# A triangular inverse by sixteen-row blocks in a hybrid decoder layer

## Chip, cores and metric

The kernel runs on one core of a Trainium2 chip. The metric is device time in microseconds of one execution; lower is better. TensorE is called PE, VectorE DVE, ScalarE ACT, GpSimd POOL, and SyncE, which issues most DMAs, SP.

## What is computed

One layer of a decoder with three parallel mixers (A: gated DeltaNet, B: RG-LRU, C: gated linear attention) between a common input projection and a common output projection, then a gated feed-forward block; 2048 prompt tokens and 64 sample tokens, float32. The change lies in mixer A, which treats chunks of 64 tokens for each of six heads:

```python
kk = jnp.einsum('bhid,bhjd->bhij', ki, ki)
lhs = eye + bi[..., :, None] * kk * dec_strict            # 64 x 64, unit lower triangular
rhs = jnp.concatenate([bi[..., None] * vi, (bi * jnp.exp(gcum))[..., None] * ki], axis=-1)
sol = lax.linalg.triangular_solve(lhs, rhs, left_side=True, lower=True, unit_diagonal=True)
u, wk = sol[..., :dv], sol[..., dv:]
w = u - jnp.einsum('bhik,bhkv->bhiv', wk, S)
qk = jnp.einsum('bhid,bhjd->bhij', qi, ki) * dec_incl
o = jnp.exp(gcum)[..., None] * jnp.einsum('bhik,bhkv->bhiv', qi, S) + jnp.einsum('bhij,bhjv->bhiv', qk, w)
S_new = jnp.exp(g_last)[..., None] * S + jnp.einsum('bhjk,bhjv->bhkv', k_dec, w)   # to the next chunk
```

## The kernel before

The program runs in stretches: the input projection (matmuls into `pm`, to about 530 us), mixer A, mixer C beside the output projection, and the feed-forward block.

Mixer A (`deltanet`) takes its 33 chunks (32 of the prompt, one that holds the 64 sample tokens) in nine batches: eight of four chunks and the sample batch. Batches go in pairs; the last pair has the sample batch as a third member. For each pair the program is written as: `prep` of its batches, `inverse` of the pair, `ahead` (some steps of the gates' projection), `blocks` of its batches, then for each batch `tokens`, `weights` and `chain`.

- `prep`: chunk decays (PE `pcl`, line 792 and 797), exponents (PE `pa`, DVE `ex`, ACT `ex` and `eb`), and for each pair of heads the scores (PE `pk`, line 837), which DVE multiplies into `LT` (the strictly triangular matrix L, line 839) and `R` (line 842). Loads of keys and queries (`kq`, `kbd`) are issued on SP one batch ahead.
- `inverse`: ACT copies the 32 x 32 diagonal blocks of L to `X0` (named `Xd`, line 888), DVE transposes them so that each partition (a lane) holds one 32 x 32 block (`Y`, line 891). Then forward substitution: in step j a column of L times row j of the result (`tmp`, line 895) is subtracted from the rows below (`Tm`, line 897). It takes 31 steps of two DVE instructions; a pair has 96 blocks of 32 rows, 24 on each group of 32 partitions (27 in the last pair), which are called quadrants here. Two transposes give the inverse back with rows on partitions in both orientations: `Tt`, which is the tile `Y` again (line 898), and `Ut` (line 899). Then PE multiplies the off-diagonal block with it (`pp`, line 906) and ACT copies the product to `Ps`.

```python
for j in range(31):
    k = 31 - j
    t = tmp[:, :k * (j + 1)].rearrange("p (a b) -> p a b", a=k)
    nc.vector.tensor_tensor(t, Y[:, j + 1:, j:j + 1].to_broadcast([128, k, j + 1]),
                            Tm[:, j:j + 1, :j + 1].to_broadcast([128, k, j + 1]), op=OP.mult)
    nc.vector.tensor_tensor(Tm[:, j + 1:, :j + 1], Tm[:, j + 1:, :j + 1], t, op=OP.subtract)
nc.vector.transpose(Tt, Tm.rearrange("p i j -> p j i"))
nc.vector.transpose(Ut.rearrange("p a b -> p (a b)"), Tm.rearrange("p a b -> p (a b)"))
```

- `blocks`: ACT copies `Ut` into `WU` (line 920), PE makes the block off the diagonal (`pu`, line 930), ACT copies it (line 934).
- `tokens`: PE transposes keys and values (`pt`, `pv`), DVE scales them to `KB`, `KD` and `X`. `weights`: PE `pw` (line 944), ACT to `WU`.
- `chain`: the recurrence. For each chunk PE `cw` (line 962), an ACT copy to `X` (line 963), PE `cw` (line 965), an ACT copy to the next chunk's `X` (line 972); then the output `po`. For every two chunks a head norm follows, an alternation of DVE (`ob`, `z`, `e`), ACT (`z`) and PE (`po` with `ones`).

Beside all this `gates` projects the gates of mixers A and C: 1152 matmuls into `zp` (lines 1121 to 1123), whose operands are loaded by SP, split by ACT (`xh`) and POOL (`xl`, line 1089). They have no tie to the inverse and fill PE.

The order of the work on each engine in mixer A is not written out by hand. A scheduler lays the program's instructions out before the launch, by their place in the program and its own costs, and each engine then runs its list in order. PSUM has eight banks; tiles with the tag "t" (`pp`, `pu`, `pt`, `pv`, `pw`) share two of them, `zp` has one.

Of the kernel before, what the change touches and what calls it, by code (L numbers as in the profile page):

```python
# [16 lines left out]
T = 2048  # L17
# [82 lines left out]
def _build_consts():  # L100
    """Selectors and masks that follow from the shapes."""
# [21 lines left out]
    add("lns", lns)  # L123
    add("lnb", lns * EPS)
# [10 lines left out]
    # sixteen of each 32 rows are kept; selA and selB take both parts of split rows  # L135
# [4 lines left out]
    # token-major columns: 0-2 -C of head 2p | 3-5 -C of head 2p+1 | 6-11 ln beta  # L140
    # | 12-17 A | 18-23 gl-g+lrk
# [39 lines left out]
def pack(inp):  # L181
    """Lay the inputs out for the chip: permutations, transposes and zero padding only."""
# [84 lines left out]
# ---------------------------------------------------------------- the chip  # L267
# [45 lines left out]
def mm3(nc, ps, wh, wl, xh, xl, first=True, last=True, by_k=False):  # L313
    """float32 product from three single passes over exactly split operands (lists over K)."""
    n = len(wh)
    seq = [(wh, xh), (wl, xh), (wh, xl)]
    order = [(a, k) for k in range(n) for a in range(3)] if by_k else [(a, k) for a in range(3) for k in range(n)]
    for i, (a, k) in enumerate(order):
        w, x = seq[a]
        nc.tensor.matmul(ps, w[k], x[k], start=first and i == 0, stop=last and i == 3 * n - 1)  # L320


def phase1(E):
    nc, tc, s, col = E.nc, E.tc, E.s, E.col
    with ExitStack() as ctx:
# [24 lines left out]
        def first_w():  # L350
            """the first tile in two parts, the second beside the first of the tokens"""
# [32 lines left out]
        def log1p(u, e, t, w):  # L384
            """u = ln(1 + e) for 0 <= e <= 1 with the rounding of 1 + e made good; t, w scratch"""
# [78 lines left out]
        def post_packed():  # L464
            """rates and decays of mixer A, a row for each head and block of tokens"""
# [56 lines left out]
        def conv(ps, nb, key, sst, ocol, taps, bias):  # L522
            """causal width-4 convolution of a block; returns a [128, n] tile"""
# [184 lines left out]
def deltanet(E, ctx, pools, need, ahead):  # L708
    """Gated DeltaNet: chunks of 64 tokens, all six heads. Operands are made for batches of four chunks,
    the triangular systems are solved for two batches at once."""  # L710
# [15 lines left out]
    LTs = [pool.tile([128, 3, 2 * CH + 1, 64], F32, name=f"LT{i}") for i in range(2)]  # L726
    X0 = inv.tile([128, 32, 32], F32, name="Xd")
    Y = inv.tile([128, 32, 32], F32, name="Y")
    Tm = inv.tile([128, 32, 32], F32, name="Tm")
    tmp = inv.tile([128, 16 * 17], F32, name="tmp")  # L730
    Ut, Tt = inv.tile([128, 32, 32], F32, name="Ut"), Y
# [50 lines left out]
    def shared(g):  # L782
        """per-token columns and chunk decays"""
# [30 lines left out]
    def decay(g, p):  # L814
        """exponents of the decay between tokens of a chunk, masked"""
# [28 lines left out]
    def prep(g):  # L844
        """decays and scores of a batch"""
# [6 lines left out]
    def tokens(g):  # L852
        """keys and values with tokens on the partitions"""
# [25 lines left out]
    def inverse(gs):  # L879
        """U = ((I + L)^-1)^T per chunk and head; 32 x 32 diagonal blocks by substitution, a lane each,  # L880
        and the first product for the block off the diagonal"""
# [3 lines left out]
        for q in range(4):  # L885
            r = slice(q * 32, (q + 1) * 32)
# [3 lines left out]
        nc.gpsimd.memset(Tm.rearrange("p a b -> p (a b)")[:, ::33], 1.0)  # L890
        nc.vector.transpose(Y.rearrange("p a b -> p (a b)"), X0.rearrange("p a b -> p (a b)"))
        for j in range(31):
            k = 31 - j
            t = tmp[:, :k * (j + 1)].rearrange("p (a b) -> p a b", a=k)
            nc.vector.tensor_tensor(t, Y[:, j + 1:, j:j + 1].to_broadcast([128, k, j + 1]),  # L895
                                    Tm[:, j:j + 1, :j + 1].to_broadcast([128, k, j + 1]), op=OP.mult)
            nc.vector.tensor_tensor(Tm[:, j + 1:, :j + 1], Tm[:, j + 1:, :j + 1], t, op=OP.subtract)  # L897
        nc.vector.transpose(Tt, Tm.rearrange("p i j -> p j i"))
        nc.vector.transpose(Ut.rearrange("p a b -> p (a b)"), Tm.rearrange("p a b -> p (a b)"))
# [12 lines left out]
    def blocks(g):  # L912
        """U of a batch, with its block off the diagonal"""
# [23 lines left out]
    def weights(g):  # L937
        """products of U with the keys"""
# [8 lines left out]
    def outputs(t0):  # L947
        """where the outputs of 128 tokens gather, and their gates"""
# [83 lines left out]
    C = load_consts(E, early, ["selC", "selG", "mneg", "mnegs"])  # L1032
# [38 lines left out]
def gates(E, ctx):  # L1071
    """The gates of mixers A and C before their activation; a generator of steps."""
# [10 lines left out]
    def split(h, lo, src, name):  # L1083
        """src from memory into rounded parts"""
# [82 lines left out]
def ln_stats(E, r, m, mv, st):  # L1167
    """mean and variance of the rows of r[:m] to mv[:m]"""
# [6 lines left out]
def ln_scale(E, mv, m):  # L1175
    """variances in mv[:m, ..., 1] to the factors of the layer norm"""
# [18 lines left out]
def head_norm(E, tr, po, z, gain, ones, out):  # L1195
    """out = RMS norm over each head of the rows of po, times silu(z); po and z are overwritten. The gate's
    sigmoid is exp(-ln(1 + exp(-z))), and the two logarithms share one exponential."""
# [15 lines left out]
class Gla:  # L1213
    """Gated linear attention: chunks of 64 tokens, six heads, operands made for four chunks at a time.
# [757 lines left out]
```

## Time and profile before

| | |
|---|---|
| runs, us | 3038.8, 3035.73, 3043.57; median 3038.8 |
| span of the profiled execution, us | 3039.2 |
| profiled execution's own time, us | 3039.2 (the profile gives its span alone) |
| mixer A in the trace, us | about 535 to 1012 |
| substitution (lines 895, 897) in the trace, us | first step 577.0, last 877.2 |

The profile is one execution of the program on the chip. Its lines name engine, line of the program, operation and tiles (out<-in). A wait is put down to what ended last before it. Every float32 matmul appears as two records, with a weight load each; a `zp` product is one.

### The profile page before, as it was taken

To read this page: it belongs to the slowest core of one execution; us is meant where nothing else is said; L and a number is where in the kernel's file an instruction comes from. 1 tells how busy PE (TensorE), PEld (TensorE's weight loads), DVE (VectorE), ACT (ScalarE), POOL (GpSimd) and SP (SyncE) were. 2 spreads that over 40 slices of the span, in tenths; PEclk is the share of its full clock that TensorE was granted. 3 is DMA by queue.
4 is the path that set the end of the run, shared out by engine and by line. 5 is a ranking of instruction groups with operands and counts; after the bars stand their busy time and mean duration, and the time that the engine had idled before them with its cause. 6 is when DMAs were issued, how large, how long until landed. Compare 5 with 4: busy or idle time off the path is not lost.

```text
span 3039.2 us, 44833 instructions
## 1 busy us (share of the span) xinstructions
PE 2895.7 (95%) x17755; PEld 2496.9 (82%) x17755; DVE 1597.9 (53%) x2654; ACT 1231.6 (41%) x2591; POOL 843.4 (28%) x892
## 2 busy tenths in 40 slices
PE   8999999789889899998899999999999999999998
PEld 7888789678778677776678888888889999999997
DVE  4564442587665688978533333333366444334446
ACT  4474443446665567756332222222232222222223
POOL 0000001734523545434322222222232222222224
PEclk9999999689898679999999999999999999999999
DMA  6221112433433333322431111111124111111111
GB/s 197 83 74 70 56 61 100 137 106 107 123 99 91 81 120 109 111 82 87 160 123 50 49 42 63 42 56 42 49 104 152 42 47 51 49 42 42 48 43 62
DMA packets 182106, 247.20 MB, mean 81 GB/s; under 512 B 37986, under 2 KB 147640, under 8 KB 181832
## 3 DMA queue, kind: packets, MB, share of 16 engines
q1 hardware_dynamic: 179768, 237.02, 24.2%
q0 software_dynamic: 1984, 7.12, 0.6%
q8 instruction: 140, 2.29, 0.3%
q14 instruction: 70, 0.57, 0.1%
q10 hardware_dynamic: 144, 0.20, 0.0%
HBM read 183.94 MB, written 60.08 MB: 80 GB/s over the span
## 4 chain that ended last, share of the span: by engine, by line
PE 79%; DVE 10%; ACT 4%; issue 3%; DMA 2%; POOL 2%; SPq 0%; POOLq 0%; ACTq 0%; DVEq 0%
PE pm L320 20%; PE pd L320 15%; PE pug L320 15%; PE puv L320 15%; PE s L1364 2%; PE zp L1121 1%; DVE Tm L897 1%; DVE y L1779 1%; DVE tmp L895 1%; DVE K L1337 1%; PE zp L1122 1%; ACT WU L920 1%; PE zp L1123 1%; PE pd L1861 1%; DMA fxl<-s_x1T 1%
## 5 line engine op out<-in xcount | busy, mean ns | idle before, releaser
L1715 DVE SCALAR_TENSOR_TENSOR act<-G,cols,act 128x1024 f32<-128x1024 f32 (+1 forms) x132 | 123.6, 950 | 493.5 <-ACT act L1713 491.1
L1868 DVE TENSOR_TENSOR y<-y,pd 128x512 f32<-128x512 f32 x322 | 220.9, 687 | 203.3 <-PE pd L320 196.8
L1606 POOL TENSOR_TENSOR wl_d<-ws_d,wh_d 128x1024 fp32r<-128x1024 f32 x44 | 106.2, 2415 | 571.3 <-ACT wh_d L1605 547.3
L320 PE MATMUL pd<-wh_d,hh 128*128 128x512 f32 x704 | 215.8, 391 | 4.4 <-DVE y L1868 2.6
L320 PE MATMUL pd<-wh_d,hl 128*128 128x512 f32 x704 | 215.4, 391 | 0.0
L320 PE MATMUL pd<-wl_d,hh 128*128 128x512 f32 x704 | 214.9, 390 | 0.0
L1695 ACT COPY G<-pug 128x512 f32<-128x512 f32 (+2 forms) x110 | 55.2, 503 | 386.3 <-PE pug L320 386.3
L320 PE MATMUL pug<-fxh,wh_g 128*128 128x512 f32 (+2 forms) x880 | 197.0, 352 | 5.3 <-ACT fxh L1658 2.7
L320 PE MATMUL pug<-fxl,wh_g 128*128 128x512 f32 (+2 forms) x880 | 196.6, 352 | 2.5 <-POOL fxl L1659 1.5
L320 PE MATMUL puv<-fxh,wl_v 128*128 128x512 f32 (+2 forms) x880 | 197.1, 353 | 1.1 <-POOL wl_v L1606 1.1
L320 PE MATMUL puv<-fxh,wh_v 128*128 128x512 f32 (+2 forms) x880 | 197.1, 353 | 0.0
L320 PE MATMUL puv<-fxl,wh_v 128*128 128x512 f32 (+2 forms) x880 | 196.9, 352 | 0.0
L320 PE MATMUL pug<-fxh,wl_g 128*128 128x512 f32 (+2 forms) x880 | 196.2, 352 | 0.3 <-POOL wl_g L1606 0.3
L320 PE MATMUL pm<-xh,wh 128*128 128x448 f32 (+1 forms) x800 | 181.9, 360 | 8.3 <-ACT xh L370 6.7
L1605 ACT CAST wh_d<-ws_d 128x1024 fp32r<-128x1024 f32 x44 | 45.7, 1039 | 339.1 <-PE pd L1861 174.9
L320 PE MATMUL pm<-xh,wl 128*128 128x448 f32 (+1 forms) x800 | 181.7, 359 | 0.0
L320 PE MATMUL pm<-xl,wh 128*128 128x448 f32 (+1 forms) x800 | 180.0, 358 | 0.1
L1757 DVE TENSOR_TENSOR hl<-act,hh 128x512 fp32r<-128x512 f32 (+2 forms) x110 | 124.1, 1128 | 99.5 <-ACT hh L1749 99.5
L320 PEld LDWEIGHTS pug<-fxh,wh_g 128*128 128x128 f32 x880 | 156.2, 188 | 21.7 <-ACT fxh L1658 4.3
L320 PEld LDWEIGHTS pug<-fxl,wh_g 128*128 128x128 f32 x880 | 155.7, 188 | 16.9 <-POOL fxl L1659 2.0
L320 PEld LDWEIGHTS puv<-fxh,wl_v 128*128 128x128 f32 x880 | 156.1, 189 | 15.3 <-POOL wl_v L1606 1.3
L320 PEld LDWEIGHTS pm<-xh,wh 128*128 128x128 f32 x800 | 144.6, 188 | 28.9 <-issue 10.1
(731 smaller groups left out, 6371.0 us busy)
## 6 DMA issues: line engine op xcount, KB each, us to landing
ws_d<-in_w_dn SPq DMA_DIRECT2D x44, 512.0 KB
ws_g<-in_w_up SPq DMA_DIRECT2D x43, 512.0 KB
ws_v<-in_w_up SPq DMA_DIRECT2D x43, 512.0 KB
zx<-in_xT SPq DMA_DIRECT2D x56, 256.0 KB
ws<-in_w_in SPq DMA_DIRECT2D x19, 512.0 KB
x<-in_x SPq DMA_DIRECT2D x16, 512.0 KB
s_x<-x SPq DMA_DIRECT2D x16, 512.0 KB
s_x1T<-xt SPq DMA_DIRECT2D x16, 512.0 KB
```

Of the source, the lines that this page charges most:

```text
L320: nc.tensor.matmul(ps, w[k], x[k], start=first and i == 0, stop=last and i == 3 * n - 1)
L895: nc.vector.tensor_tensor(t, Y[:, j + 1:, j:j + 1].to_broadcast([128, k, j + 1]), Tm[:, j:j + 1, :j + 1].to_broadcast([128, k, j + 1]), op ...
L897: nc.vector.tensor_tensor(Tm[:, j + 1:, :j + 1], Tm[:, j + 1:, :j + 1], t, op=OP.subtract)
L920: nc.scalar.copy(o[:, h, :, :, jh * 32:(jh + 1) * 32], Ut[r, :, :3 * mt].rearrange("p i (a c) -> p a c i", a=3)[:, :, g.c0:g.c0 + m])
L1121: nc.tensor.matmul(ps, wh[:, k], xl, start=k == 0, stop=False)
L1364: nc.tensor.matmul(ps[64:, c], K[:, i], Q[:, i], start=True, stop=True)
L1605: nc.scalar.copy(h, t)
L1606: nc.gpsimd.tensor_tensor(lo, t, h.bitcast(F32), op=OP.subtract)
L1695: nc.scalar.copy(G[:, 2 + o:2 + o + m], p[:, :m])
L1715: nc.vector.scalar_tensor_tensor(dst(act), src(i), taps[i], dst(act), op0=OP.mult, op1=OP.add)
L1757: nc.vector.tensor_tensor(dst, act[:, c], hh[:, c].bitcast(F32), op=OP.subtract)
L1868: nc.vector.tensor_tensor(y, y, ps, op=OP.add)
```

## The change

Each block of 32 rows is taken as two blocks of sixteen on its diagonal and one block of sixteen by sixteen below them. With D for the inverse of the two diagonal blocks (zero elsewhere) and N for the lower block, the inverse of the 32 rows is D - D N D. The substitution runs on both blocks of sixteen at once in the same lane, in 15 steps of two DVE instructions. D N is a round of small matmuls into `pn`, copied by ACT to `Wd` (the tile `Tm`), and its product with D is made in both orientations (`pb` for `Ut`, `pc` for `Tt`), to be subtracted by three DVE instructions. `X0` is kept for N: ACT scales its upper half of columns by a mask (`half`, one more constant to load), POOL clears the other half.

The tiles `Y` and `Tm` get 32 more elements for each lane, so that the view `diagonal` can step from one block to the other. Comments and docstrings are gone from the whole program, which moves line numbers.

```diff
+    def square(t):
+        return t[:, :1024].rearrange("p (a b) -> p a b", b=32)
+    def diagonal(t):
+        return t.rearrange("p (b x) -> p b x", b=2)[:, :, :512].rearrange("p b (i j) -> p b i j", j=32)[:, :, :, :16]
-    Y = inv.tile([128, 32, 32], F32, name="Y")
-    Tm = inv.tile([128, 32, 32], F32, name="Tm")
-    tmp = inv.tile([128, 16 * 17], F32, name="tmp")
-    Ut, Tt = inv.tile([128, 32, 32], F32, name="Ut"), Y
+    Yf = inv.tile([128, 2 * 528], F32, name="Y")
+    Tf = inv.tile([128, 2 * 528], F32, name="Tm")
+    Y, Tm, Yb, Tb = square(Yf), square(Tf), diagonal(Yf), diagonal(Tf)
+    tmp = inv.tile([128, 2 * 64], F32, name="tmp")
+    Ut, Tt, Wd = inv.tile([128, 32, 32], F32, name="Ut"), Y, Tm
...
+        quads = [slice(q * 32, (q + 1) * 32) for q in range(4)]
...
-        for j in range(31):
-            k = 31 - j
-            t = tmp[:, :k * (j + 1)].rearrange("p (a b) -> p a b", a=k)
-            nc.vector.tensor_tensor(t, Y[:, j + 1:, j:j + 1].to_broadcast([128, k, j + 1]),
-                                    Tm[:, j:j + 1, :j + 1].to_broadcast([128, k, j + 1]), op=OP.mult)
-            nc.vector.tensor_tensor(Tm[:, j + 1:, :j + 1], Tm[:, j + 1:, :j + 1], t, op=OP.subtract)
+        nc.scalar.activation(X0[:, 16:], X0[:, 16:], AF.Copy, scale=C["half"])
+        nc.gpsimd.memset(X0[:, :16], 0.0)
+        for j in range(15):
+            k = 15 - j
+            t = tmp[:, :2 * k * (j + 1)].rearrange("p (b i j) -> p b i j", b=2, i=k)
+            sh = [128, 2, k, j + 1]
+            nc.vector.tensor_tensor(t, Yb[:, :, j + 1:, j:j + 1].to_broadcast(sh),
+                                    Tb[:, :, j:j + 1, :j + 1].to_broadcast(sh), op=OP.mult)
+            nc.vector.tensor_tensor(Tb[:, :, j + 1:, :j + 1], Tb[:, :, j + 1:, :j + 1], t, op=OP.subtract)
         nc.vector.transpose(Tt, Tm.rearrange("p i j -> p j i"))
-        nc.vector.transpose(Ut.rearrange("p a b -> p (a b)"), Tm.rearrange("p a b -> p (a b)"))
+        nc.vector.transpose(Ut.rearrange("p a b -> p (a b)"), Tf[:, :1024])
+        for u0 in range(0, ns, 16):
+            w = min(16, ns - u0)
+            pn = psum(f"pn{gs[0].b}{u0}", (128, 16, 32), "t")
+            for u in range(w):
+                for r in quads:
+                    nc.tensor.matmul(pn[r, u], X0[r, :, u0 + u], Tt[r, :, u0 + u], start=True, stop=True)
+            nc.scalar.copy(Wd[:, u0:u0 + w], pn[:, :w])
+        pb = psum(f"pb{gs[0].b}", (128, 32, 16), "t")
+        for u in range(ns):
+            for r in quads:
+                nc.tensor.matmul(pb[r, u], Wd[r, u], Ut[r, 16:, u], start=True, stop=True)
+        pc = psum(f"pc{gs[0].b}", (128, 32, 16), "t")
+        for u in range(ns):
+            for r in quads[::2]:
+                nc.tensor.matmul(pc[r, u], Ut[r, :, u], Wd[r, u, :16], start=True, stop=True)
+        for r in quads[::2]:
+            nc.vector.tensor_tensor(Tt[r, :16, :ns], Tt[r, :16, :ns], pc[r, :ns].rearrange("p u j -> p j u"),
+                                    op=OP.subtract)
+        nc.vector.tensor_tensor(Ut[:, 16:, :ns], Ut[:, 16:, :ns], pb[:, :ns].rearrange("p u i -> p i u"),
+                                op=OP.subtract)
...
-    C = load_consts(E, early, ["selC", "selG", "mneg", "mnegs"])
+    C = load_consts(E, early, ["selC", "selG", "mneg", "mnegs", "half"])
```

The scheduler then lays the whole of mixer A out anew. In the rows that follow, each is line, operation, tiles and shape of what is written, with `x16` for sixteen equal ones in a row; numbers behind a name tell buffers apart. In the changed kernel lines are 9 to 33 higher than before (`ex` is line 831, `pk` 846, `pp` 939, `cw` 995 and 998).

PE at the first inverse. Before, `pp` follows a run of `zp`, of which 234 stand ahead of it:

```order
L1123 MATMUL zp_0_5912<-xh_2_5891,zh_4334 128x256
L906 MATMUL pp_4773<-Y,LT_4435 32x32 x16
L906 MATMUL pp_4792<-Y,LT_4435 32x32 x16
L1121 MATMUL zp_0_5912<-xl_3_5904,zh_4334 128x256
L1122 MATMUL zp_0_5912<-xh_3_5903,zl_4335 128x256
```

Now 150 `zp` stand ahead of `pn` (and 168 ahead of `pp`):

```order
L846 MATMUL pk_5866<-kq_5771,kbd_4432 128x128 x4
L918 MATMUL pn_4745<-Y,Xd 32x32 x64
L918 MATMUL pn_4811<-Y,Xd 32x32 x32
L1154 MATMUL zp_0_5582<-xl_1_5550,zh_4334 128x256
...
L1154 MATMUL zp_0_5582<-xl_2_5562,zh_4334 128x256
L923 MATMUL pb_4845<-Ut,Tm 32x16 x96
L927 MATMUL pc_4942<-Tm,Ut 32x16 x48
```

So 84 `zp` and 16 of the 56 `pk` that stood ahead of the end of the first substitution have moved behind it.

PE at the end of the first pair's chain, beside which the second inverse runs. Before, the second inverse's `pp` and `pu` stand within the chain (`cw`):

```order
L965 MATMUL cw_5167<-X_4421,KD_4423 64x64 x6
L977 MATMUL po_5143<-R_4416,X_4421 64x64 x6
L906 MATMUL pp_5775<-Y,LT_4436 32x32 x16
L906 MATMUL pp_5794<-Y,LT_4436 32x32 x16
...
L819 MATMUL pa_6927<-rs_6850,sel 128x256 x2
L962 MATMUL cw_5391<-X_4422,WU_4426 64x64 x6
L906 MATMUL pp_5813<-Y,LT_4436 32x32 x16
L930 MATMUL pu_6296<-Ut,Ps 32x32 x16
```

Now `pn`, `pb` and `pc` stand there, and `pp` behind the chain's last `cw`:

```order
L923 MATMUL pb_6066<-Ut,Tm 32x16 x13
L927 MATMUL pc_6163<-Tm,Ut 32x16 x10
L998 MATMUL cw_5691<-X_4422,KD_4424 64x64 x6
L1010 MATMUL po_5667<-R_4417,X_4422 64x64 x6
L927 MATMUL pc_6163<-Tm,Ut 32x16 x29
L1239 MATMUL po_5667<-z_5668,c_ones 128x384
L927 MATMUL pc_6163<-Tm,Ut 32x16 x9
...
L846 MATMUL pk_7354<-kq_7259,kbd_4433 128x128 x4
L828 MATMUL pa_7367<-rs_7290,sel 128x256 x2
L939 MATMUL pp_6215<-Y,LT_4436 32x32 x16
```

The second half of the chain has no `zp` beside it any more; `pp`, `pu`, the next pair's `prep` and the tokens of the pair itself come after it.

DVE at the same place. Before, the transposes that end the second inverse stand ahead of the chain's second norm (`ob`, `z`, `e`):

```order
L897 TENSOR_TENSOR Tm<-Tm,tmp 128x31
L898 STREAM_TRANSPOSE Y<-Tm 128x1024
L899 STREAM_TRANSPOSE Ut<-Tm 128x1024
L842 TENSOR_TENSOR R_4416<-pk_6891,ex_6884 64x256 x2
L842 TENSOR_TENSOR R_4416<-pk_6914,ex_6907 64x256 x2
L1204 TENSOR_TENSOR ob_5188<-po_5143,z_5144 128x384
```

Now the subtractions that end it stand within the chain's fourth and last norm:

```order
L1237 TENSOR_TENSOR ob_5712<-po_5667,z_5668 128x384
L1241 SCALAR_TENSOR_TENSOR z_5668<-e,z_5668 128x384
L929 TENSOR_TENSOR Y<-Y,pc_6163 32x16x24 x2
L931 TENSOR_TENSOR Ut<-Ut,pb_6066 128x16x24
L1234 TENSOR_SCALAR e<-z_6880 128x384
```

Its transposes come 25 rows earlier, ahead of the first norm; the subtractions have moved behind the last one's `z`, which waits for ACT.

More of the change, by code (lines that the diff above doesn't have):

```diff
@@ L123, in _build_consts @@
     add("lns", lns)
+    add("half", p % 32 < 16)
     add("lnb", lns * EPS)
@@ L884, in inverse @@
         LT = gs[0].LT
-        for q in range(4):
-            r = slice(q * 32, (q + 1) * 32)
+        quads = [slice(q * 32, (q + 1) * 32) for q in range(4)]
+        for q, r in enumerate(quads):
             o = (q % 2) * 32
@@ L889, in inverse @@
         nc.gpsimd.memset(Tm, 0.0)
-        nc.gpsimd.memset(Tm.rearrange("p a b -> p (a b)")[:, ::33], 1.0)
-        nc.vector.transpose(Y.rearrange("p a b -> p (a b)"), X0.rearrange("p a b -> p (a b)"))
-        for j in range(31):
-            k = 31 - j
-            t = tmp[:, :k * (j + 1)].rearrange("p (a b) -> p a b", a=k)
-            nc.vector.tensor_tensor(t, Y[:, j + 1:, j:j + 1].to_broadcast([128, k, j + 1]),
-                                    Tm[:, j:j + 1, :j + 1].to_broadcast([128, k, j + 1]), op=OP.mult)
-            nc.vector.tensor_tensor(Tm[:, j + 1:, :j + 1], Tm[:, j + 1:, :j + 1], t, op=OP.subtract)
@@ L898, in inverse @@
-        nc.vector.transpose(Tt, Tm.rearrange("p i j -> p j i"))
-        nc.vector.transpose(Ut.rearrange("p a b -> p (a b)"), Tm.rearrange("p a b -> p (a b)"))
+        nc.gpsimd.memset(Tf[:, :1024:33], 1.0)
+        nc.vector.transpose(Yf[:, :1024], X0.rearrange("p a b -> p (a b)"))
+        nc.scalar.activation(X0[:, 16:], X0[:, 16:], AF.Copy, scale=C["half"])
[7 more added lines that the diff above has]
+            nc.vector.tensor_tensor(Tb[:, :, j + 1:, :j + 1], Tb[:, :, j + 1:, :j + 1], t, op=OP.subtract)
```

## The prediction

> **What bounds the kernel now.** I read the page first, then the busy time by stage, then the chain of waits in three stages, then single rows.
>
> ```profile
> span 3039.2 us, 44833 instructions
> PE 2895.7 (95%) x17755; PEld 2496.9 (82%) x17755; DVE 1597.9 (53%) x2654; ACT 1231.6 (41%) x2591; POOL 843.4 (28%) x892
> ```
>
> Over the whole span PE is the bound. The change lies in mixer A, about 535 to 1012 us, so that stretch decides. I cut it where the state chain of each pair of batches issues its first cw matmul: 667.0, 742.6, 833.3 and 928.0 us. This view gives busy time by stage; the seven stages are called P, I, B and 0 to 3 here.
>
> ```profile
> core 0: us, PE busy (x) PEld busy (x) DVE busy (x) ACT busy (x) POOL busy (x), PEclk, DMA share, GB/s
> 535.00:575.00 40.00, 30.54 (x192) 28.56 (x192) 11.73 (x25) 18.73 (x36) 31.15 (x33) 0.63 0.54 154
> 575.00:632.00 57.00, 40.97 (x284) 38.17 (x284) 51.30 (x92) 23.95 (x50) 32.79 (x37) 0.79 0.40 115
> 632.00:667.00 35.00, 31.45 (x392) 28.65 (x392) 26.58 (x57) 19.42 (x42) 10.53 (x12) 0.80 0.32 93
> 667.00:742.60 75.60, 70.94 (x883) 63.43 (x881) 51.40 (x96) 48.91 (x95) 27.25 (x27) 0.95 0.35 99
> 742.60:833.30 90.70, 78.17 (x902) 70.13 (x901) 68.87 (x124) 58.11 (x118) 47.56 (x66) 0.89 0.43 123
> 833.30:928.00 94.70, 84.61 (x952) 74.73 (x951) 63.45 (x138) 59.59 (x160) 31.13 (x40) 0.92 0.37 105
> 928.00:1012.00 84.00, 79.91 (x785) 69.93 (x784) 33.83 (x70) 41.29 (x119) 31.08 (x33) 0.88 0.27 77
> ```
>
> Two things are to be seen. In stage I (the first inverse) DVE is busy 51.3 of 57 us and PE stands for 16 us: DVE is the bound. In stages 0 to 2 PE is busy 70.9 of 75.6, 78.2 of 90.7 and 84.6 of 94.7 us, so it stands for 4.7 + 12.5 + 10.1 = 27.3 us only, although DVE is loaded too. The chain of waits says how much of those stages the substitution (lines 895 and 897) holds:
>
> ```profile
> by line: ACT WU L920 9.1%; DVE Tm L897 8.3%; ACT Xd L888 8.1%; PE zp L1121 7.2%; PE cw L962 6.9%; PE zp L1122 6.3%; DVE tmp L895 6.1%; PE zp L1123 6.0%; PE pw L944 4.6%; PE pk L837 4.1%; PE cw L965 3.1%; PE po L1206 3.1%; PE pu L930 3.0%; P
> by line: ACT WU L920 7.6%; ACT Xd L888 7.4%; DVE Tm L897 6.7%; issue 6.1%; PE pw L944 5.8%; PE zp L1121 5.2%; PE cw L965 5.0%; PE zp L1122 5.0%; PE cw L962 4.8%; PE zp L1123 4.6%; DVE tmp L895 4.0%; PE pu L930 3.4%; PE pt L870 3.0%; DMA zx<
> by line: DVE tmp L895 12.0%; DVE Tm L897 11.4%; issue 7.5%; PE zp L1121 6.7%; ACT WU L920 6.4%; PE zp L1122 5.4%; PE zp L1123 5.3%; PE cw L962 3.5%; DMA q<-s_cq 3.5%; PE cw L965 2.6%; DVE KB L871 2.2%; DVE X L877 2.1%; DVE KD L872 1.9%; DVE
> ```
>
> These are stages 0, 1 and 2: 14.4% of 75.6, 10.7% of 90.7 and 23.4% of 94.7 us, which is 10.9 + 9.7 + 22.2 = 42.8 us.
>
> **The change part by part.** *Substitution.* By line, and four rows of the view that keeps shapes apart:
>
> ```profile
> L895 DVE TENSOR_TENSOR tmp<-Y,Tm 128x31 f32<-128x31 f32 (+15 forms) x124 | 67.1, 541 | 3.6
> L897 DVE TENSOR_TENSOR Tm<-Tm,tmp 128x31 f32<-128x31 f32 (+15 forms) x124 | 64.3, 519 | 3.6
> L895 DVE TENSOR_TENSOR tmp<-Y,Tm 128x112 f32<-128x112 f32 x8 | 5.2, 644 | 0.2
> L897 DVE TENSOR_TENSOR Tm<-Tm,tmp 128x112 f32<-128x112 f32 x8 | 3.1, 392 | 0.2
> L895 DVE TENSOR_TENSOR tmp<-Y,Tm 128x87 f32<-128x87 f32 x8 | 2.1, 257 | 0.2
> L897 DVE TENSOR_TENSOR Tm<-Tm,tmp 128x87 f32<-128x87 f32 x8 | 2.0, 249 | 0.2
> ```
>
> Now: (67.1 + 64.3) / 4 = 32.9 us for each of four inverses, in 62 instructions. After: 30 instructions of 30 to 128 elements, 91 in the mean, which lies between the last four rows; their mean is 386 ns, so 30 x 0.386 = 11.6 us.
>
> *First inverse, on the path.* The time at which it ends now, and the first cw:
>
> ```profile
> 630.14 1.92 DVE L898 STREAM_TRANSPOSE Y<-Tm 128x1024 f32<-128x1024 f32 x1
> 631.98 1.20 DVE L899 STREAM_TRANSPOSE Ut<-Tm 128x1024 f32<-128x1024 f32 x1
> 632.11 1.98 PE L906 MATMUL pp<-Y,LT 32*32 32x32 f32 x64 [2.94 <-DVE Y L898]
> 667.04 0.45 PE L962 MATMUL cw<-X,WU 128*64 128x64 f32 x4
> 592.83 0.41 DVE L839 TENSOR_TENSOR LT<-pk,ex 128x256 f32<-128x256 f32 x1
> ```
>
> In the new DVE order an LT product of the next pair, the one that ran at 592.8, stands ahead of the last seven steps. It waits for a pk that the change does not hasten, so I leave it there: 592.8 + 1.3 (LT and R) + 7 x 0.39 + 3.1 (transposes) = 600. Then come pn, its copy, pb and pc, priced below at 3.8 + 0.7 + 3.8 + 3.0, and three subtractions. Their nearest row is a DVE product from PSUM with as many columns:
>
> ```profile
> L1204 DVE TENSOR_TENSOR ob<-po,z 128x384 f32<-128x384 f32 x14 | 7.7, 550 | 12.9 <-PE po L977 10.3 <-DMA s_mix<-ob 2.5
> ```
>
> 3 x 0.55 = 1.7, and with a microsecond and a half of hand-overs the first pp comes at 614.5 instead of 632.1: a gain of 17.6 us. Bounds: 9, with small matmuls at the higher price below (4.4 more) and hand-overs of 2 us; 21, with the lower price and steps of 0.25 us.
>
> *The new small matmuls.* Nearest row: pp above, whose loop alternates two heads on two 32x32 tiles: 1.98 us for 64 records, 31 ns each (a program's matmul is two records). pn and pb alternate four quadrants. Bounds: 31 ns, if four go no faster than two, and 15, if they go twice as fast. I take 20, nearer to the second, because the loop is of the same kind, only wider. An inverse has 2 x 192 records of pn and pb and 96 of pc on two quadrants: 384 x 0.020 + 96 x 0.031 = 10.7 us, between 8.8 and 14.9; the last one, with 27 systems, 12.0. [...] No row here shows four side by side.
>
> *Moved zp products* (the gates' projection, filler on PE). How many ran in each stage from I on:
>
> ```profile
> 575.00:632.00 57.00, 26.01 (x150) 0.79 0.40 115
> 632.00:667.00 35.00, 14.56 (x78) 0.80 0.32 93
> 667.00:742.60 75.60, 29.23 (x190) 0.95 0.35 99
> 742.60:833.30 90.70, 28.41 (x164) 0.89 0.43 123
> 833.30:928.00 94.70, 43.57 (x282) 0.92 0.37 105
> 928.00:1012.00 84.00, 31.84 (x204) 0.88 0.27 77
> 926.56 0.28 PE L1122 MATMUL zp<-xh,zl 128*128 128x256 f32 x1
> 926.68 0.28 PE L1123 MATMUL zp<-xh,zh 128*128 128x256 f32 x1
> 583.10 1.13 PE pk L837 x8
> ```
>
> Counted in the new order between the same events: 84, 96, 186, 174, 384, 144. One zp takes 0.12 us of the queue (two starts above), four pk 1.13. So stage B gets 18 zp and 8 pk more: +4.4 us. The first cw comes 17.6 - 4.4 = 13 us earlier. Stage 0: 10.7 (small matmuls) - 0.5 (4 zp less) + 3.4 (12 pk more) + 1.0 (8 pa of 0.12) = +14.6. Stage 1: 10.7 + 1.2 - 2.2 - 0.5 = +9.2. Stage 2: 12.0 + 102 x 0.12 = +24.2. Stage 3: -60 x 0.12 = -7.2. Since PE is busy over 86% of these stages, I count all of it on the path: +40.8.
>
> *Relief of DVE in stages 0 to 2.* Of the 42.8 us on the chain 11.6/32.9 remain, so 27.7 go; that is also the idle time PE has (27.3). Late next: in the new order the subtractions of inverses 1 to 3 stand on DVE behind the norms of the chain before, and pp, pu and the tokens behind them, since pb and pc hold both "t" buffers of PSUM.
>
> ```profile
> DVE z L1208 <- ACT z L1207: 35.4, 6, 12.1
> ```
>
> Such a wait is 5.9 us in the mean; PE has the rest of pc, 7 zp, 4 pk and 2 pa in its queue ahead of pp, some 4 us. I lose 2 us at each of three: relief 22. Bounds: 9 and 42.8.
>
> *At nothing:* the scaled copy, the copies of pn and the earlier refill of X0 on ACT, the memset on POOL, and one load of 128 numbers (`half`) on SP's queue behind four others of its kind, long before the first inverse uses it. ACT is free for 15.6 us in stage B and 27 to 35 in 0 to 2, POOL for 43 or more; without that cover the refill costs stage B its length.
>
> ```profile
> L888 ACT COPY Xd<-LT 32x768 f32<-32x768 f32 (+1 forms) x16 | 25.2, 1575 | 1.9 <-DVE LT L839 1.7
> ```
>
> That is 4 x 1.575 = 6.3 us.
>
> Sum: -13.1 + 40.8 - 22 = +5.7. Against the profiled execution, 3039.2 us, that is 3044.9; this execution lies 0.4 us above the median of the three runs, 3038.8, so 3045.
>
> **The rivals.** *DVE was the true bound of stages 0 to 2* (faster). For it: 23.4% of stage 2's chain is substitution and DVE is busy 68.9 of 90.7 us in stage 1. Then all 42.8 us go, and with four quadrants side by side the matmuls cost 8 us less in four inverses: 5.7 - 20.8 - 8 = -23, or 3016. It decides as soon as relief passes 37 us. Against it: PE stands for only 27.3 us there.
>
> *PE pays in full* (slower): 31 ns a record costs 4.2 us more per inverse, 17.4 in all, and the waits of DVE behind the norms leave 9 of relief: 5.7 + 17.4 + 13 = +36, or 3075. For it: PE's 90% in stages 0 to 2; against it: part of that is the modelled end of a matmul (0.28 us shown, 0.12 between starts).
>
> *Each change of tile form stops PE.* The zp behind small matmuls takes longer than its successor:
>
> ```profile
> 880.73 0.39 PE L1121 MATMUL zp<-xl,zh 128*128 128x256 f32 x1
> 880.95 0.28 PE L1122 MATMUL zp<-xh,zl 128*128 128x256 f32 x1
> ```
>
> 0.22 instead of 0.12 us to the next start. The new order has some 53 pieces of pn, pb and pc between wider matmuls; at 0.1 to 0.2 each, 5 to 11 us more: 3050 to 3056. [...]
>
> *The first inverse isn't released earlier,* because pn stands in PE's queue behind pk and zp whose operands are late. PE stood for 16 us in stage I, not all of it for DVE. Then the 13 us are not had: 3058.
>
> **How the numbers follow.** A measurement of this kernel can tell 0.3%, 9.1 us: 3029.7 to 3047.9 counts as no change. My forecast has 0.42 (own range 3028 to 3058: 0.03 faster, 0.27 same, 0.12 slower), DVE-bound 0.26 (0.25 faster, 0.01 same), PE in full 0.18 (slower), tile form 0.07 (0.01 same, 0.06 slower), no earlier release 0.07 (0.02 same, 0.05 slower). Together 0.28 faster, 0.31 same, 0.41 slower. The range of 3016 to 3072 leaves out the far halves of the two outer cases, under 0.2.
>
> **What would show it.** Lines 908 and 910: 60 + 60 records and about 46 us instead of 131; the first pp near 614 and the first cw near 654 us; pn and pb at 15 to 31 ns a record; stages 0 and 2 longer by 5 to 15 us, with the gap between the end of a chain and the next first cw grown and the chain itself shorter; stage 3 shorter by about 7. The prediction is wrong if stages 0 to 2 together get shorter (DVE did bound them), or if the records of pn cost over 31 ns.

## The result, and the profile after

The change is slower: 3062.2 us (median; 3056.2 to 3070.9) against 3037.5 us, a ratio of 1.0088 with a 95% interval of 1.0067 to 1.011. The forecast was 3045 us. The profiled execution is the slowest of the four, so the spans lie further apart (29.9 us) than the medians (24.8). The page of the changed kernel, span and busy time of each engine:

```profile
span 3069.1 us, 48712 instructions
PE 2930.3 (95%) x19735; PEld 2533.0 (83%) x19735; DVE 1527.0 (50%) x2538; ACT 1240.0 (40%) x2603; POOL 840.6 (27%) x896
```

DVE has 70.9 us less work than before, PE 34.6 us more, and the span grew by 29.9 us. Busy time by stage, cut at the same events as before (first pp at 615.9, first cw of each pair at 657.5, 755.0, 849.6 and 964.1, last group of cw at 1042.1 us):

```profile
core 0: us, PE busy (x) PEld busy (x) DVE busy (x) ACT busy (x) POOL busy (x), PEclk, DMA share, GB/s
535.00:575.00 40.00, 30.00 (x193) 27.95 (x193) 11.87 (x24) 18.90 (x38) 30.90 (x33) 0.67 0.54 153
575.00:616.00 41.00, 32.95 (x646) 30.90 (x648) 28.82 (x54) 13.51 (x30) 18.95 (x24) 0.76 0.33 91
616.00:657.50 41.50, 34.61 (x438) 32.44 (x435) 24.15 (x45) 26.62 (x52) 15.91 (x20) 0.84 0.37 105
657.50:755.00 97.50, 90.03 (x1436) 80.99 (x1434) 56.40 (x106) 56.37 (x116) 37.02 (x40) 0.89 0.36 100
755.00:849.60 94.60, 84.60 (x1345) 76.12 (x1343) 38.79 (x70) 55.93 (x110) 33.45 (x35) 0.93 0.35 99
849.60:964.10 114.50, 107.22 (x1586) 96.24 (x1585) 42.55 (x109) 63.86 (x161) 41.19 (x61) 0.91 0.37 105
964.10:1042.10 78.00, 73.76 (x745) 64.78 (x743) 38.48 (x81) 41.66 (x128) 38.38 (x50) 0.87 0.26 76
```

The first cw comes 9.5 us earlier. Stages 0 to 2 take 306.6 instead of 261.0 us, stage 3 takes 78 instead of 84. Together 30.1 us, which is the whole difference of the spans. In stages 0 to 2 DVE's load fell from 183.7 to 137.7 us. PE's rose from 233.7 to 281.9 us, and its idle time fell from 27.3 to 24.8 us only. So PE's queue got longer by 48.1 us, and 46.0 us less work on DVE bought 2.5 us of PE's idle time.

The chain itself did get shorter; the time went behind it. The last copy of the state in the first chain and the next first cw, after:

```profile
704.12 0.47 ACT L1005 COPY X<-cw 64x384 f32<-64x384 f32 x1 [1.24 <-PE cw L998]
755.04 0.45 PE L995 MATMUL cw<-X,WU 128*64 128x64 f32 x4
```

and the same two events before:

```profile
736.69 0.46 ACT L972 COPY X<-cw 64x384 f32<-64x384 f32 x1
742.55 0.68 PE L962 MATMUL cw<-X,WU 128*64 128x64 f32 x8
```

A chain that ended 70 us behind its first cw now ends after 47, and the gap behind it grew from 6 to 51 us. Here the shorter chain was no gain, since PE's queue had the same work left behind it.

### The profile page after: what moved, and what is told of

The parts are those of the page before. It is cut to its first block, busy times and chain, and to the rows that moved or that the text cites. A ratio compares the mean times of both kernels' runs of the same rounds, so it can differ in the third digit from the quotient of the medians.

```text
span 3069.1 us, 48712 instructions
## 1 busy us (share of the span) xinstructions
PE 2930.3 (95%) x19735; PEld 2533.0 (83%) x19735; DVE 1527.0 (50%) x2538; ACT 1240.0 (40%) x2603; POOL 840.6 (27%) x896
## 4 chain that ended last, share of the span: by engine, by line
PE 79%; DVE 9%; ACT 4%; issue 3%; DMA 3%; POOL 2%; SPq 0%; POOLq 0%; DVEq 0%; ACTq 0%
PE pm L321 20%; PE pd L321 15%; PE pug L321 15%; PE puv L321 15%; PE s L1397 2%; PE zp L1154 1%; DVE y L1812 1%; DMA zx<-in_xT 1%; PE zp L1156 1%; ACT WU L953 1%; PE zp L1155 1%; DVE K L1370 1%; PE pd L1894 1%; PE cw L995 1%; PE po L1239 1%
## 5 line engine op out<-in xcount | busy, mean ns | idle before, releaser
L321 PEld LDWEIGHTS pug<-fxh,wh_g 128*128 128x128 f32 x880 | 155.9, 188 | 17.6 <-ACT wh_g L1638 3.0
L321 PEld LDWEIGHTS puv<-fxh,wh_v 128*128 128x128 f32 x880 | 156.3, 188 | 13.9
```

## The experiments

Three theories are weighed. Theory 1: the new records on PE are simply paid, since PE bounds stages 0 to 2. Theory 2: the loss comes from the order, because the tail of an inverse (pn, pb, pc, pp, pu) now stands late, its end behind the chain. Theory 3, formed after eight runs: time on PE is its records plus its waits plus the clock that it loses, and a wait counts only where it ends at the substitution.

The table has each kernel's median, the 95% interval of its ratio to runs of the kernel before that were taken beside it (their medians: 3034.6 to 3037.5 us), and from the view of busy time the stretch from 535 us to the last po record of mixer C's samples, called the mark below: its length, PE's busy and idle time in it, and the mean granted clock of PE. Up to 50 more records of mixer C's s lie ahead of the mark in some kernels; that is 2 to 5 us of PE's busy time.

| kernel | us | ratio (95%) | stretch | PE busy | PE idle | PEclk |
|---|---|---|---|---|---|---|
| before | 3037.5 | | 540.8 | 471.7 | 69.1 | 0.83 |
| change | 3062.2 | 1.0067–1.011 | 570.6 | 507.2 | 63.4 | 0.84 |
| e1 tail first | 3055.3 | 1.0046–1.0078 | 561.3 | 493.6 | 67.7 | 0.85 |
| e2 no D N D | 3004.0 | 0.9882–0.9917 | 509.8 | 455.4 | 54.4 | 0.86 |
| e3 no subtraction | 3066.1 | 1.0081–1.0117 | 568.5 | 503.2 | 65.3 | 0.85 |
| e4 before + matmuls | 3089.3 | 1.0144–1.0187 | 590.0 | 515.1 | 74.9 | 0.82 |
| e5 first pair only | 3044.6 | 1.0018–1.0039 | 543.9 | 469.6 | 74.3 | 0.85 |
| e6 relief, pairs 1–3 | 3043.6 | 1.0015–1.0039 | 547.2 | 468.7 | 78.5 | 0.84 |
| e7 transpose for pc | 3047.4 | 1.0025–1.005 | 553.6 | 488.6 | 65.0 | 0.86 |
| e8 e5 + order | 3038.2 | 1.0000–1.0017 | 543.2 | 473.6 | 69.6 | 0.85 |
| e9 relief, first pair | 3031.2 | 0.9976–0.9999 | 534.7 | 466.3 | 68.4 | 0.83 |
| e10 more DVE work | 3061.4 | 1.0075–1.0101 | 568.9 | 488.9 | 80.0 | 0.81 |
| e11 before + order | 3054.5 | 1.0044–1.0073 | 562.3 | 491.5 | 70.9 | 0.80 |
| e12 e7 + order | 3050.6 | 1.0029–1.006 | 557.7 | 490.3 | 67.5 | 0.84 |

**e1, the tail first.** `tc.high_priority()` has the scheduler plan these instructions ahead of others.

```diff
+        with tc.high_priority():
             nc.vector.transpose(Tt, Tm.rearrange("p i j -> p j i"))
...
                 nc.scalar.copy(Ps[r, u0:u0 + w], pp[r, :w])
```

> The change with the same instructions, but everything from the two transposes after the substitution to the copies of pp planned at high priority. In the changed kernel the first pp of inverses 1 to 3 stands behind the last (96th) cw of the chain before, with 48 pn, 96 pb and 48 pc around cw 42 to 90; here it stands behind the 48th, 48th and 35th cw. Theory 1 (the 32 us of new PE work are simply paid, because PE is the bound of stages 0 to 2): order is worth nothing, 3062 us within 8, stages 0 to 2 together still about 306 us. Theory 2 (the tail of the inverse stands behind the chain, so that tail, pu, pw and tokens lie open between two chains): 20 to 40 us come back, 3022 to 3042 us, the gap from the last X copy of a chain to the next first cw shrinks from 52 to 64 us to 30 or less.

3055.3 us: 7 below the change, with intervals that overlap. The tail ran amid the chain as meant, and the gap behind the first chain shrank from 51 to 11 us, but the chain grew from 47 to 81: stages 0 to 2 took 295.3 us, 11 less. This order wins back only a small part of the loss, where theory 2 had 20 to 40 us.

**e2 and e3, the new work left out, and its result unused.**

```diff
-            pn = psum(...)   # and pb, pc, the copies, `half`
...
-        for r in quads[::2]:
-            nc.vector.tensor_tensor(Tt[r, :16, :ns], Tt[r, :16, :ns], pc[r, :ns]..., op=OP.subtract)
-        nc.vector.tensor_tensor(Ut[:, 16:, :ns], Ut[:, 16:, :ns], pb[:, :ns]..., op=OP.subtract)
```

e2 takes out all of it, e3 only the three subtractions.

> The change without pn, pb, pc, their copies and subtractions: the part D N D of each 32-row block is left out. Theory 1: 3062 less some 32 us of PE work, about 3030 us, stages 0 to 2 about 274 us. Theory 2: the work and the late tail go together, so at least 45 us less, 3000 to 3020 us, since the shorter substitution then shows its relief of 20 us or more. If DVE had no share in the bound at all, stages 0 to 2 come out as before (261 us) and only the first inverse is earlier (by 20 to 25 us): 3012 to 3018 us.

> The change with pn, pb and pc computed but not subtracted (D N D is left out of the result), so that pp waits for neither DVE nor pc's result. The first pp still stands behind the 96th cw, since pb and pc hold the same two PSUM buffers. Theory 1: 3062 us within 8 (same PE work). Theory 2 by place in PE's queue: 3050 to 3062 us, the same gaps. A third theory, that the time is lost in the wait of pp for the subtractions on DVE behind the norms: 3030 to 3045 us, with gaps shorter by 6 us or more each.

e3 is no faster than the change (3066.1), so the wait of pp for DVE carries none of the loss. e2 is 62.1 us faster than e3, with the same substitution: leaving out pn, pb and pc is worth more than the whole loss. Its 3004.0 us lie 26 below theory 1's number and within theory 2's range, because more than the records goes with them: in the table PE's busy time differs by 47.9 us and its idle time by 10.9. Stages 0 to 2, e2 first, then e3:

```profile
640.20:899.70 259.50, 244.18 (x2854) 218.33 (x2852) 135.57 (x287) 169.78 (x383) 111.20 (x136) 0.95 0.42 120
656.30:965.20 308.90, 286.45 (x4410) 257.84 (x4409) 134.12 (x285) 176.94 (x389) 113.29 (x138) 0.92 0.36 103
```

PE is busy 42.3 us more in e3. Less 61 zp of 0.12 us that e3 has more there, this is 35.0 us for three inverses, against the forecast's 33.4. And e2 shows what the shorter substitution is worth without them: with 48 us less for DVE, stages 0 to 2 took 259.5 us against 261.0 before, 77 more zp among them; PE idled 15.3 us instead of 27.3.

**e4, the new matmuls added to the kernel before.**

```diff
         nc.vector.transpose(Ut.rearrange("p a b -> p (a b)"), Tm.rearrange("p a b -> p (a b)"))
+        ...pn, pb, pc as in the change, from X0, Tt, Tm and Ut, with no copies and no subtraction
```

> The kernel before with its 62-step substitution, and pn, pb and pc added after the transposes with results that nothing uses. The first pp moves behind the 90th to 96th cw (before: 48th to 78th). Theory 1: 32 us of PE work added, 3066 to 3074 us, spread over all four inverses. Theory 2: the work alone fills idle time of PE in stage I, and what is lost is lost in stages 0 to 2 where the gap after a chain grows by the place of pp: 3050 to 3066 us.

3089.3 us, 53.5 above before, more than both expected. PE's busy time rose by 43.4 us, 1.9 of it for 50 more s records (forecast for four inverses: 10.7 x 3 + 12.0 = 44.1), its idle time by 5.8. The rest of the difference lies behind the mark or in the spread of single profiles.

With the kernel before (3035.8 beside them), e2, e3 and e4 form a square of short or long substitution, with or without the small matmuls. The matmuls (in e3 with their copies) cost 53.5 us with the long one and 62.1 with the short one. The short substitution saves 31.7 us without them and 23.1 with them. That is about the lead at the first cw: it comes 26.8 us earlier in e2 than before, and 22.8 earlier in e3 (656.3) than in e4 (679.1). Stages 0 to 2 keep the lead: they take about as long as with the long substitution (e4: 305.0 us), although more zp are left for them, 77 in e2 and 99 in e3. PE's idle time in them falls by 12.0 us in e2 and by 8.1 in e3 against e4, and the relief of DVE is worth no more than that there. After these four runs theory 1 had the cause, at too low a price, and theory 2 had lost most of its share.

**e5 and e6, the two halves of the change apart.** e5 keeps the new inverse for the first pair alone; e6 leaves the first as before and gives the other three the 15 steps.

```diff
+        if gs[0].pair == 0:      # e6: != 0, without pn, pb and pc
             for j in range(15):
...
+        else:
+            for j in range(31):  # as before
```

> The new inverse (15 steps and D N D) for the first pair of batches alone, where PE stands; the 62-instruction substitution as before for the other three. Theory 1 (PE's queue bounds stages 0 to 2, DVE bounds only the first inverse): first cw near 657 us as in the change, stages 0 to 2 together 261 to 268 us as before, so 3036 - 10 = 3026 us, between 3020 and 3034: faster than both kernels. Theory 2 (the shorter substitution was worth the 22 us of the forecast in stages 0 to 2 and the loss came from the order): taking it back there costs these 22 us, so 3040 us or more.

> The mirror image without new work: the first inverse as before, and for the other three the 15 steps alone, without pn, pb and pc (D N D is left out there). It measures the relief of DVE in stages 0 to 2 by itself. By the forecast's term: 22 us, 3036 - 22 = 3014 us, first cw at 667. Theory 1 by the run that left D N D out of all four (stages 0 to 2 at 264 us there, with 77 zp products more, against 261): 5 to 10 us, 3026 to 3031 us. DVE as the true bound: 43 us, 2993 us.

3044.6 and 3043.6 us, each 8 to 9 us slower than before. Theory 1 missed both. e5 came out where theory 2 had it (3040 or more), but e6 takes away the reason that theory 2 gave: the relief by itself was to bring 3014 us. e6 shows the relief alone, by stage 0 to 2 and, last, from the last group of cw to the mark:

```profile
667.40:738.60 71.20, 66.38 (x859) 59.78 (x857) 32.65 (x59) 46.48 (x91) 23.54 (x23) 0.98 0.36 104
738.60:824.50 85.90, 80.48 (x915) 70.40 (x914) 46.43 (x84) 52.54 (x117) 43.01 (x45) 0.94 0.44 126
824.50:913.70 89.20, 76.13 (x896) 67.65 (x894) 50.39 (x114) 61.01 (x152) 35.02 (x65) 0.91 0.36 100
...
994.10:1082.20 88.10, 70.27 (x500) 56.47 (x499) 62.96 (x130) 48.30 (x147) 44.40 (x78) 0.58 0.37 100
```

DVE is busy 129.5 us in stages 0 to 2 instead of 183.7, and PE idles 23.3 instead of 27.3: 54 us off DVE bought 4.0 us of PE's idle time. These stages are 14.7 us shorter, but mostly because 66 zp were left for later. 49 zp ran in the last row, at a granted clock of 0.58, beside the start of mixer C. That stretch was this long before:

```profile
1012.00:1076.00 64.00, 55.29 (x389) 41.31 (x389) 54.37 (x124) 39.83 (x119) 29.02 (x58) 0.58 0.38 110
```

All of the gain and more was given back there: 24 us.

**e7, fewer records.**

```diff
-        pc = psum(f"pc{gs[0].b}", (128, 32, 16), "t")
-        ...its matmuls and two subtractions
+        nc.vector.transpose(Tt.rearrange("p j u -> p u j"), Ut.rearrange("p i u -> p u i"))
```

> The change without the 396 records of pc and their two subtractions per inverse: Tt is made from the finished Ut by one more transpose on DVE (1.2 to 1.9 us each). Theory 1 (records on PE are paid by their time in PE's queue, 9.3 us of pc in stages 0 to 2 and 2.8 in the first inverse): 9 to 13 us less than the change, 3049 to 3053 us. If the waits of pp for DVE carried the loss: 3060 us or more, since DVE has 1 us more per inverse between pb and pp.

3047.4 us, 15 below the change, though DVE has an instruction more between pb and pp: records on PE are what counts, as theory 1 has it. PE's busy time fell by 18.5 us, of which the 396 records of pc are 12.8 by their row below.

**e8 and e11, order alone.**

```diff
+            with tc.high_priority():
                 ...the two transposes, pp and its copies, unchanged
```

e8 is e5 with that edit, e11 is before with it.

> The new inverse for the first pair alone, and the transposes and pp of the other three planned at high priority (their first pp stands behind the 66th, 36th and 66th cw of the chain instead of the 66th, 36th and 96th). Theory 1: order changes PE's work by nothing, 3026 us as with the new inverse for the first pair alone, within 6. Theory 2: the last gap shrinks by 10 us or more, 3010 to 3020 us.

> The kernel before, with the transposes, pp and its copies planned at high priority, no other change. The first pp of inverses 1 to 3 stands behind the 42nd, 54th and 90th cw instead of the 48th, 72nd and 78th. If order alone is worth the 6 us by which the two kernels with the new inverse for the first pair differed, 3030 us; if that was chance of the order, within 5 us of 3036.

e8 is 6 us faster than e5 and equal to before; e11 is 18 us slower than before. Every expected time missed. The edit helps two kernels by 6 to 7 us (e1, e8) and harms another by 18, as much as the effects that e5 and e6 were to show. In e11 PE's waits hardly changed (idle 70.9 against 69.1), and its busy time grew by 19.8 us with 49 s records more ahead of the mark (4818 records against 4769): its granted clock was 0.80, 0.83 before. Stage 3 shows it most. With 84 zp fewer than before (120 against 204) and 60 other records more, PE was busy 87.3 us there instead of 79.9:

```profile
952.30:1041.40 89.10, 87.30 (x761) 77.16 (x760) 43.67 (x84) 40.24 (x117) 32.90 (x42) 0.70 0.17 48
```

Before, with 204 zp, the clock there was 0.88. In e10, with 60, it was 0.72; in three kernels with 216 (e1, e5, e12) 0.96 to 0.98. That the filler keeps up the clock fits these rows. It is loose elsewhere: the four kernels with 144 (change, e3, e4, e7) had 0.85 to 0.94, e6 with 222 had 0.90, and no run varied the filler alone.

**e9, an early first inverse for nothing.** The 15 steps for the first pair without pn, pb and pc, the rest as before (the e5 edit, without its matmuls).

> The 15 steps alone for the first inverse (D N D left out there), the other three as before. Theory of the forecast (DVE bounds stage I, so an earlier first inverse is a gain): the first pp 30 us earlier, the first cw 25 us earlier, of which at least 15 us stay: 3021 us or less. Theory 3 (only waits of PE can be saved, and in the trace of before only 2.9 us of PE's waits in stage I end at the inverse; the rest of its queue is work that has to be done later): the first cw comes 25 us earlier, stage 0 gets longer by nearly as much, 3026 to 3036 us.

The first cw came 25.3 us earlier, and the end 5.4 us (ratio 0.9987). Stages P to B and stage 0:

```profile
535.00:641.70 106.70, 83.27 (x743) 77.77 (x743) 57.32 (x110) 55.49 (x110) 63.57 (x72) 0.74 0.44 125
641.70:741.80 100.10, 86.53 (x993) 76.97 (x991) 81.23 (x149) 55.42 (x117) 41.23 (x42) 0.88 0.39 109
```

Up to the first cw PE was busy 83.3 us instead of 103.0: 77 zp (235 against 312) and other work simply weren't done yet. Stage 0 took 100.1 us instead of 75.6. The time is what theory 3 expected, and most of stage 0's growth is PE's own work moved behind the chain's start. But PE also idled 13.6 us there instead of 4.7, and the largest wait is for the end of the next, long substitution:

```profile
PE pp L927 <- DVE Y L919: 4.4, 1, 4.4
```

Another 4.2 us went to pp behind Ps. So with the chain earlier, DVE did hold PE up (it was busy 81.2 of 100.1 us), and a lead that e2 keeps is lost here.

**e10, more work for DVE.**

```diff
             nc.vector.tensor_tensor(t, Y..., Tm..., op=OP.mult)
+            if gs[0].pair > 0:
+                nc.vector.tensor_tensor(t, Y..., Tm..., op=OP.mult)
```

> The kernel before, with the first instruction of each substitution step issued twice in inverses 1 to 3: 31 more instructions of 541 ns, 16.8 us more of DVE in each of stages 0 to 2, nothing else. If the chain of waits priced the substitution rightly (14 to 23% of these stages), DVE's extra work is paid by half or more: 25 to 50 us more, 3060 us or above. Theory 3 (PE's queue covers DVE in these stages; no wait of PE in 667 to 928 us ended at the substitution): at most 12 us more, 3036 to 3048 us.

3061.4 us, 24.7 above before: at the lower edge of the first expectation (3060 or above), and theory 3's "at most 12" missed. Stages 0 to 2:

```profile
666.30:760.70 94.40, 84.26 (x958) 75.16 (x956) 77.74 (x151) 54.53 (x110) 37.81 (x36) 0.87 0.37 105
760.70:860.70 100.00, 84.49 (x952) 75.65 (x950) 77.87 (x150) 57.64 (x115) 44.76 (x62) 0.95 0.38 111
860.70:958.40 97.70, 84.07 (x967) 74.49 (x965) 68.67 (x147) 60.38 (x160) 34.23 (x39) 0.95 0.38 110
```

DVE has 40.6 us more (224.3), PE idles 39.3 instead of 27.3. So DVE is not free either: 41 us added cost 12.0 us of idle PE, while 54 us taken away (e6) gave 4.0. That is less than a third of the added work, not the half or more that the chain of waits would have. The kernel before seems to stand near the point where DVE's load begins to tell (e2, with 48 us less, gained 12.0, so the point isn't sharp). These three stages also ran 144 zp more than before (780 against 636). Stage 3 had as many fewer and still took 87.5 us instead of 84, at a clock of 0.72.

**e12, both improvements of the change.** The edit of e7, with the tail planned at high priority.

> The change with both edits that lowered it: the transpose of Ut in place of pc (15 us less) and the tail at high priority (7 us less). The first pp of inverses 1 to 3 stands behind the 54th, 48th and 54th cw, and 216 zp products are left for stage 3 (138 with the transpose alone, 204 before). If the two savings add: 3062 - 22 = 3040 us. Theory 3, that PE's time is its records plus its waits plus the clock it loses, makes the same sum: records 26 us above before, waits at best 5 below it: 3036 + 21 - 17 (filler left for stage 3, by the 16 us of clock that the kernels without it lost there) is the lower end, 3040, and 3057 the upper. If order is chance: above 3047 us.

3050.6 us: not below e7, within theory 3's range and also where chance of the order would put it. The savings did not add, and no version of the full change beat the kernel before.

What stays open: e2 is 32 us faster than before, while its two halves give 5 us of gain (e9) and 8 us of loss (e6). Its stretch has 14.7 us less idle PE and 16.3 us less busy time at a clock of 0.86. Two losses of the halves are missing in its trace: no wait of PE in stages 0 to 2 ends at the substitution (e9 has 4.4 us), and no zp is left behind the last group of cw (e6 has 49). So the halves need each other, but whether these two make up the difference no run shows.

## Why the prediction was right or wrong

The measured time lies 17 us above the forecast and inside the stated range, and the direction was right. By terms, on the spans: the earlier first cw brought 9.5 us (forecast 13.1), PE's added work cost 42.1 (40.8), the relief brought 2.5 (22). So nearly all of the miss is one term, and the range held because it made room for the rival *PE pays in full*, not because that term was near.

*Substitution and first inverse.* Lines 908 and 910, and the three small matmuls:

```profile
L908 DVE TENSOR_TENSOR tmp<-Y,Tm 128x30 f32<-128x30 f32 (+7 forms) x60 | 27.6, 459 | 2.0
L910 DVE TENSOR_TENSOR Tm<-Tm,tmp 128x30 f32<-128x30 f32 (+7 forms) x60 | 26.3, 438 | 1.8
L918 PE MATMUL pn<-Y,Xd 32*32 32x32 f32 x792 | 16.5, 227 | 2.8 <-DVE Y L911 2.8
L927 PE MATMUL pc<-Tm,Ut 32*32 32x16 f32 x396 | 12.8, 205 | 0.0
L923 PE MATMUL pb<-Ut,Tm 32*32 32x16 f32 x792 | 12.6, 191 | 2.4 <-issue 2.4
```

53.9 us instead of 46, since an instruction took 449 ns in the mean and not 386. The first pp came at 615.9 (forecast 614.5), the first cw at 657.5 (forecast 654): right to 1.4 and 3.5 us. (The lower bound of this gain, 9 us, doesn't follow from what it is said to be made of: 17.6 less 4.4 and half a microsecond is 12.7. No later sum names it.) The rival "not released earlier" fell.

*Small matmuls.* Records that alternate four quadrants start closer together than those of pp, which alternate two heads. The tile view of the first pn, and of the first pp before:

```profile
L918 PE MATMUL pn<-Y,Xd x192: 223/223/253, 599.6 to 602.3; 32*32 32x32 f32 x192
L906 PE MATMUL pp<-Y,LT x64: 218/228/229, 632.1 to 633.9; 32*32 32x32 f32 x64
```

192 records in 2.7 us are 14 ns each from start to start, where two heads took 28 (31 with the end of the last record). The lower bound was right in such a burst. For the 1980 records the rows above have 41.9 us, forecast 44.1; but they count the modelled end of each record (0.2 us) too. Counted in the trace from each start to the next start on PE, whatever that is, the same records take 37.6 us, and the lower bound (8.8 for an inverse) makes 36.3. Within a piece the price is nearly the same at a granted clock of 1.00 and of 0.50: pn starts every 15 and every 14 ns, pc every 29 and 28. So the price of 20 ns was too high for the records themselves. *PE pays in full* was wrong on the price and nearer the truth on relief (9).

*Moved zp and the sum of PE's work.* The counts of moved zp came out to the last one, and the sum looks exact: forecast for stages 0 to 2 +14.6, +9.2 and +24.2 = 48.0 us, and PE's busy time there rose by 48.1. Stage 3's length fell by 6.0, forecast 7.2. But that the sum is so close is luck. By stage the busy time rose by 19.1, 6.4 and 22.6 us. Counted from start to start, the small records took 29.7 us (forecast 33.4), the zp, 108 more of them, 17.3 more (forecast 12.9) and the rest 1.2 more (forecast 1.7). That is 0.16 us for each zp added, not 0.12: these stages ran 54.6 us at a granted clock of 0.50, 41.0 before, and the prediction has no term for the clock. *Each change of tile form stops PE* showed as a later start only, and a small one: 17 zp stand directly behind a piece of pn, pb or pc, and their next start comes 0.10 us later than behind another zp (0.16 at a granted clock of 0.50), 2 us in all. What other matmuls pay behind such a piece isn't counted here.

*Relief of DVE.* Here the prediction failed: 22 us forecast, 2.5 had; in the other pairs 4.0 (e6), 8.1 (e3 against e4) and 12.0 (e2). The step that failed was to read the relief from the chain of waits (42.8 us on lines 895 and 897) and to let it take all of PE's 27.3 us of idle time. A view that the prediction didn't use comes nearer: PE's own waits in stages 0 to 2 of the kernel before.

```profile
engine line waited for: us in total, times, longest us
PE pt L870 <- issue: 5.1, 2, 3.1
PE pk L837 <- DVE R L842: 4.4, 1, 4.4
PE po L1206 <- ACT z L1205: 4.0, 2, 2.5
PE cw L962 <- ACT X L972: 2.9, 3, 2.4
PE pw L944 <- DVE KD L872: 1.9, 2, 1.5
PE pv L875 <- ACT WU L934: 1.8, 1, 1.8
PE zp L1121 <- ACT zo L1127: 1.6, 1, 1.6
PE pv L875 <- DVE X L877: 1.4, 2, 0.9
PE pw L944 <- ACT WU L945: 1.3, 1, 1.3
PE cw L965 <- ACT X L963: 0.8, 1, 0.8
PE pt L870 <- DMA kv<-s_k: 0.7, 1, 0.7
```

No wait in it ends at Y, Tm or Ut; 7.7 us end at DVE at all (R, KD, X), between what e6 and e2 got. The longest of these, 4.4 us, goes back to the substitution even so: on DVE R stood behind its last steps, with one instruction of a norm between, while pk stood on PE.

```profile
788.78 0.18 DVE L897 TENSOR_TENSOR Tm<-Tm,tmp 128x31 f32<-128x31 f32 x1
789.46 0.86 DVE L842 TENSOR_TENSOR R<-pk,ex 64x256 f32<-64x256 f32 x2
790.37 1.65 PE L837 MATMUL pk<-kq,kbd 128*128 128x128 f32 x6 [4.39 <-DVE R L842]
```

So a wait has to be followed one step further, to what the engine was doing just before. In the rest of the three stages the chain passes through the substitution while PE had other work. In stage I the same view has 2.9 us for pp behind Y, not the 16 us that PE stood there; the other waits end at eb, zo, xl, eg and R.

*DVE was the true bound* fell with this: 54 us off DVE gave 4.0 us of PE's idle time, and 48 us in e2 gave 12.0, where the rival had 42.8. e9 and e10 show that with an earlier chain or more load DVE begins to bind.

## What to carry to other kernels

Where an engine is fed by filler, price the relief of another engine by the first one's own waits (which of them end at the relieved engine, and what that engine was doing just before), not by that work's share of the chain or by the idle time as a whole. Price added work on the full engine at its records, all of them, and expect more: here 44 us of records in the forecast cost 53.5 to 62.1 us of time, with idle time and clock. A mere change of order moved this kernel by 6 to 18 us, so an effect below that needs more than one version to be believed.

## What the runs showed of the hardware

A stretch of stage 0 in the changed kernel, in rows of 3.4 us, with the granted clock of PE behind its busy time:

```profile
714.30:717.70 3.40, 2.93 (x26) 1.00 0.37 101
717.70:721.10 3.40, 2.43 (x83) 1.00 0.20 46
721.10:724.50 3.40, 3.40 (x28) 0.50 0.40 114
724.50:727.90 3.40, 2.08 (x22) 0.50 0.55 175
727.90:731.30 3.40, 1.55 (x34) 0.50 0.00 0
731.30:734.70 3.40, 3.40 (x30) 0.50 0.10 23
734.70:738.10 3.40, 3.09 (x26) 0.99 0.75 209
```

The second row, in which PE waited for 1 us, has a clock of 1.00, and the four rows behind it have 0.50. In two of the four PE is busy throughout: behind the first of these the clock was still 0.50, behind the other 0.99. In the rows at 0.50 two zp start 0.21 us apart, in the first row, at 1.00, 0.12:

```profile
715.22 0.28 PE L1155 MATMUL zp<-xh,zl 128*128 128x256 f32 x1
715.34 0.28 PE L1156 MATMUL zp<-xh,zh 128*128 128x256 f32 x1
725.32 0.41 PE L1155 MATMUL zp<-xh,zl 128*128 128x256 f32 x1
725.53 0.41 PE L1156 MATMUL zp<-xh,zh 128*128 128x256 f32 x1
```

In the traces of the kernel before and of the changed one, from 535 to 1060 us, the granted clock falls from 1.00 to 0.50 36 times and comes back 37 times. In the 3.4 us ahead of a fall PE waited for 1.46 us in the mean, against 0.41 for each 3.4 us of the whole stretch; ahead of six of the falls it waited for less than 0.17. In the 3.4 us ahead of a return it waited for 0.03 us in the mean and 0.35 at most. So in these kernels a wait on PE can cost more than its length, and kernels with nearly the same records (4769 in e9, 4818 in e11) differ by 25 us in PE's busy time (466.3 and 491.5, 4.8 of it on s) at granted clocks of 0.83 and 0.80.
